# A seven-product MLP step on one Trainium2 core: the order of work where the last up task meets the first down pair

## The chip, the cores and the metric

The kernel runs on one core of one Trainium2 chip. The metric is the device time of one execution in microseconds (us), the median of several runs. Matrix products run on TensorE (PE in the profile; PEld is its weight load), elementwise work on VectorE (DVE), ScalarE (ACT) and GpSimd (POOL); SyncE (SP) issues DMAs. Each engine works through its own list of instructions in order.

## The reference, cut to what matters

A two-layer encoder step over 512 prompt frames and 64 sample frames (576 tokens, model width 1024). Layer 0 mixes by causal pooling, layer 1 by sparse attention; each is followed by a squared-ReLU MLP of width 4096. The change lies in the MLP, which runs once in each layer:

```python
def _mlp(h, w_up, w_down):
    u = jax.nn.relu(h @ w_up)
    return (u * u) @ w_down

def _trunk(x, ...):
    for i in range(DEPTH):                      # DEPTH = 2
        h = _rmsnorm(x, norm_mix[i])
        ...                                     # pooling or attention
        x = x + y.astype(x.dtype)
        x = x + _mlp(_rmsnorm(x, norm_mlp[i]), mlp_w_up[i], mlp_w_down[i]).astype(x.dtype)
    return (_rmsnorm(x, norm_final), ...)
```

## The kernel before

**Layout.** Everything is transposed: 128 features lie on the partitions, 576 tokens in the free dimension, cut into two halves of 288. float32 operands are split in a rounded part and a rest (`upper` is ScalarE's cast, `lower` VectorE's subtraction), and a product is three matmuls: both parts of the data with the weights' rounded part, the data's rounded part with the weights' rest.

**Seven products.** A pair of weight blocks times the two token halves is a 2 by 2 block product; `seven` forms it with seven products in place of eight. Seven weight combinations ("weight units") meet seven combinations of the data (the factors b11, t1, t2, b21, t3, b22, t4, in the order in which they are used). A product (`product`) is four K-tiles ("rows" 0 to 3) of three matmuls each, 12 matmuls of 128x288. The results gather in three PSUM banks: b takes b11 and t2, then t3, then t4; c takes t1, then b22; a starts as ScalarE's copy of b11 out of bank b (L530) and takes b21. Between two products of one bank an engine must read the bank: `on.c`, `on.b`, `on.lo0`, `on.hi1`, `on.hi0`, `on.lo1` name these reads.

**Up and down.** The hidden width is done in four chunks. Chunk 0 goes up by plain products. For chunks 1 to 3 there are four up tasks (class `Up`, data from `xs` and `xt`), whose outputs are scaled, rectified, squared (`relu`, L592 on VectorE, then the square on ScalarE, L451) and combined to the seven factors of the next stage in a tile v; their parts go to a tile u. Then come four down pairs (class `Down`), whose rows 0 to 3 are the u tiles of the four up tasks, and which add to the residual x (L559). In the last chunk of the last layer there are three down pairs, and a plain ending (`last`) for the rest.

**The transition.** The last up task of a chunk (`self.final`) makes row 3 of all seven factors. The first down pair after it (`late`) does rows 0 to 2 of t1 and t2 first. There are six such transitions, three in each layer. In the up task, `hi1` adds the saved t1 part of bank c to bank b after t3 (L609) and so frees bank b for t4; `hi0` does the same for bank c (L615); `lo0` reads bank a; `lo1` reads bank b after t4. All four hang on VectorE. v has one buffer, u has four.

**What sets the order.** In this part no order is written out. A scheduler with estimated durations picks, for each engine, the next instruction that it takes to be ready, in the order of the program where several are. Weight units are made by a generator: `ahead()` asks for one more (ScalarE's cast L181, VectorE's subtraction L182, and between them the sums L260 and L264 for the combinations), up to five ahead of use. So the casts and subtractions of weights stand in the same lists as the work on v and u. SyncE and GpSimd issue the weights' DMAs as their buffers come free.

Of the kernel before, what the change touches and what calls it, by code (L numbers as in the profile page):

```python
# [22 lines left out]
HT = T // 2  # L23
# [33 lines left out]
def pool_dsa_kernel(ctx: ExitStack, tc: tile.TileContext, a, o):  # L57
# [339 lines left out]
    def mlp(layer, gi, late=0, end=None):  # L397
# [69 lines left out]
                    phase["u"].tile([P, 7, 2, HT], F32R, tag="u", bufs=4, name=uid("u")))  # L467

        def upper(u, v, f):
            act.copy(u[:, f, 0], v[:, f])  # L470

        def lower(u, v, f):
            dve.tensor_tensor(u[:, f, 1], v[:, f], f32(u[:, f, 0]), ALU.subtract)  # L473

        def parts_of(u, v, f):

            upper(u, v, f)
            lower(u, v, f)

        def first_sum(v):  # L480
            dve.tensor_tensor(v[:, 2], v[:, 4], v[:, 1], ALU.subtract)

        def middle_sums(v):
            dve.scalar_tensor_tensor(v[:, 3], v[:, 5], -1.0, v[:, 2], ALU.mult, ALU.subtract)
            dve.tensor_tensor(v[:, 1], v[:, 5], v[:, 1], ALU.subtract)

        def last_sum(v):
# [8 lines left out]
        def product(bank, w, operand, factor, js, first=False):  # L496
            for j in js:
                wh, wl = (t[:, j * P:(j + 1) * P] for t in w)
                uh, ul = (operand(j, factor, part) for part in range(2))
                for i, (wt, ut) in enumerate(((wh, uh), (wh, ul), (wl, uh))):  # L500
                    pe.matmul(bank[:, :HT], wt, ut, start=first and j == 0 and i == 0, stop=j == 3 and i == 2,  # L501
                              skip_group_check=True)

        tasks = [0]

        def ahead(n=1):

            how["sub"] = dve
            for _ in range(n):
                if len(ready) < LEAD:  # L510
                    u = next(units, None)
                    if u is not None:
                        ready.append(u)

# [5 lines left out]
        def seven(operand, late, on):  # L520


            b, a_, c = (psum1(t) for t in "bac")
            on.banks = [t[:, :HT] for t in (a_, b, c)]
            w = take()
            product(b, w, operand, "b11", rows, True)
            tasks[0] += 1
            if tasks[0] <= SEEDED:
                pe.matmul(a_[:, :HT], w[0][:, :P], operand(0, "b11", 0), start=True, stop=True, skip_group_check=True)
            act.copy(a_[:, :HT], b[:, :HT])  # L530
            ahead()
            w1 = take()
            if late:
                w2 = take()
                product(c, w1, operand, "t1", rows[:3], True)
                product(b, w2, operand, "t2", rows[:3])
                product(c, w1, operand, "t1", rows[3:])
                on.c()
                ahead()
                product(b, w2, operand, "t2", rows[3:])  # L540
            else:
                product(c, w1, operand, "t1", rows, True)
                on.c()
                ahead()
                product(b, take(), operand, "t2", rows)
            on.b()
            ahead()
            for bank, factor, then in ((a_, "b21", on.lo0), (b, "t3", on.hi1), (c, "b22", on.hi0), (b, "t4", on.lo1)):
                product(bank, take(), operand, factor, rows)
                then()  # L550

        class Down:


            def __init__(self, q):
                self.lo, self.hi = ([x[2 * q + i][:, c0:c0 + HT] for i in range(2)] for c0 in (HT, 0))

            def update(self, to, bank, op):
                dve.tensor_tensor(to, to, self.banks[bank], op)  # L559

            def c(self):
                self.update(self.hi[1], 2, ALU.subtract)

            def b(self):
                self.update(self.hi[0], 1, ALU.add)
# [16 lines left out]

        class Up:


            def __init__(self, c, j):
                self.at, self.final = (c, j), j == half - 1
# [18 lines left out]

            def hi1(self):
                v = self.v
                dve.tensor_tensor(v[:, 5], self.banks[1], snap[:, 0], ALU.add)  # L609
                self.relu(5, v[:, 5], ALU.min, 0)  # L610
                ahead()

            def hi0(self):
                v = self.v
                dve.tensor_tensor(v[:, 1], self.banks[2], snap[:, 1], ALU.add)  # L615
                self.relu(1, v[:, 1], ALU.max, 0)
                if end and self.at[0] == 3:
                    left_over(self.at[1], v[:, 1])
                parts_of(self.u, v, slice(5 if self.final else 4, 6))
                first_sum(v)  # L620
                middle_sums(v)

            def lo1(self):
                v = self.v
                self.relu(6, self.banks[1], ALU.min, 1)
                if not self.final:
                    ahead()
                parts_of(self.u, v, slice(1, 4))
                last_sum(v)
                if not self.final:  # L630
                    ahead()
                parts_of(self.u, v, slice(0, 7, 6))
                if self.final:
                    ahead(2)

        def spread():

# [76 lines left out]
        if end:  # L714
            rest = []
            for j in range(half):
                if j % 2 == 0:
                    t = x_sums_tile()
                rest.append(t[:, j % 2])
                split(rest[j], parked[j // 2][:, j % 2, :HT])  # L720
            b11, b22, b21 = ([u[:, FACTORS.index(f)] for u in us] for f in ("b11", "b22", "b21"))
            end([rest + b22, b11 + b21])

# [856 lines left out]
```

## Time and profile before

| what | value |
|---|---|
| median of 3 runs | 1086.31 us (1084.51 to 1087.21) |
| the profiled execution's own time | 1086.18 us |
| its span, first to last instruction | 1084.4 us |
| PE, busy | 1052.2 us, 97% |
| DVE, busy | 905.4 us, 83% |
| ACT, busy | 627.7 us, 58% |
| POOL, busy | 263.9 us, 24% |
| mean granted TensorE clock | 0.994 |

The page of the profile gives busy times by engine, the chain of work that ended last, and the costliest groups of instructions. The views of the trace list waits by engine (who waited for whom, total, times, longest), instructions in order of time with the idle time ahead of them in brackets, and busy times with the granted clock in stretches of the span. A matmul's listed length is about 0.29 us, but matmuls follow each other every 0.13 us; the end of one is modelled.

### The profile page before, as it was taken

The numbers are of one execution on the slowest core, as the hardware profiler recorded it, in microseconds if no ns is written. First come the engines' busy times: TensorE is split into PE (matmuls) and PEld (weight loads), VectorE is DVE, ScalarE is ACT, GpSimd is POOL, SyncE is SP. The second block draws the span as 40 slices with busy tenths as digits, with TensorE's granted clock in tenths as the row PEclk, the third lists the DMA queues.
The fourth block names the chain that finished last, engine by engine and source line by source line (L and its number), as shares of the span: only waits on it lengthen the run. The fifth ranks groups of instructions, "written<-read, shape, count | busy, mean of one in ns | idle before, by whom it ended". The sixth has DMA issues, their size and how long they took to land.

```text
span 1084.4 us, 21653 instructions
## 1 busy us (share of the span) xinstructions
PE 1052.2 (97%) x7942; PEld 1024.4 (94%) x7942; DVE 905.4 (83%) x1837; ACT 627.7 (58%) x1240; POOL 263.9 (24%) x285
## 2 busy tenths in 40 slices
PE   9999999999999999999989999999999999999996
PEld 8999999999999999999979888999999999999895
DVE  7889889879978987869998944689889879979974
ACT  8556457447546654444477776456467447547641
POOL 3200111111111100227687892000111111111001
PEclk9999999999999999999999999999999999999998
DMA  8233776676676654456642454443775776676512
GB/s 252 91 100 89 173 163 160 162 164 165 154 165 166 156 161 165 126 155 186 200 113 66 136 161 127 126 108 89 175 162 150 172 167 164 152 170 157 128 50 88
DMA packets 94460, 157.66 MB, mean 145 GB/s; under 512 B 13730, under 2 KB 25297, under 8 KB 94353
## 3 DMA queue, kind: packets, MB, share of 16 engines
q1 hardware_dynamic: 68720, 109.80, 33.1%
q0 software_dynamic: 15840, 28.84, 17.4%
q10 hardware_dynamic: 9792, 17.63, 5.3%
q8 instruction: 62, 1.02, 0.4%
q14 instruction: 46, 0.37, 0.1%
HBM read 141.15 MB, written 10.89 MB: 140 GB/s over the span
## 4 chain that ended last, share of the span: by engine, by line
PE 78%; DVE 8%; DMA 4%; ACT 3%; issue 3%; POOL 2%; SPq 1%; DVEq 0%; POOLq 0%; ACTq 0%
PE b L501 29%; PE c L501 15%; PE up L305 9%; PE a L501 7%; PE pj L305 5%; PE wo L305 2%; PE wa L305 2%; DVE wl L182 2%; PE pb L1005 1%; PE pt L1304 1%; PE sc L1278 1%; PE o L1336 1%; PE dn L305 1%; DMA raw<-in_w_in 1%; DMA raw<-in_w_down 1%
## 5 line engine op out<-in xcount | busy, mean ns | idle before, releaser
L181 ACT CAST wh<-raw 128x512 fp32r<-128x512 f32 (+1 forms) x316 | 194.8, 620 | 250.8 <-PE b L501 84.4
L182 DVE TENSOR_TENSOR wl<-raw,wh 128x512 fp32r<-128x512 f32 (+1 forms) x294 | 206.1, 703 | 38.6 <-ACT wh L181 29.2
L501 PE MATMUL b<-u,wh 128*128 128x288 f32 x992 | 202.2, 296 | 3.6 <-ACT a L530 3.2
L501 PEld LDWEIGHTS b<-u,wh 128*128 128x128 f32 x992 | 159.0, 188 | 6.0 <-ACT a L530 6.0
L181 ACT CAST wh<-sum 128x512 fp32r<-128x512 f32 x165 | 101.7, 620 | 81.3 <-PE b L501 42.3
L501 PE MATMUL b<-u,wl 128*128 128x288 f32 x496 | 145.3, 295 | 0.0
L182 DVE TENSOR_TENSOR wl<-sum,wh 128x512 fp32r<-128x512 f32 x165 | 111.9, 687 | 26.3 <-ACT wh L181 24.0
L238 POOL DMA_DIRECT2D sum<-in_w_down x31 | 27.1, 891 | 329.0 <-DVE u L473 119.3
L501 PE MATMUL c<-u,wh 128*128 128x288 f32 x496 | 102.8, 296 | 0.1
L501 PEld LDWEIGHTS b<-u,wl 128*128 128x128 f32 x496 | 92.9, 188 | 0.0
L305 PE MATMUL up<-xs,wh 128*128 128x288 f32 x512 | 89.6, 296 | 0.9 <-DVE x L1471 0.8
L501 PE MATMUL b<-xt,wh 128*128 128x288 f32 x384 | 78.2, 297 | 6.7 <-DVE v L609 6.7
L473 DVE TENSOR_TENSOR u<-v,u 128x864 fp32r<-128x864 f32 (+2 forms) x100 | 81.7, 824 | 0.5 <-ACT u L470 0.5
L501 PEld LDWEIGHTS c<-u,wh 128*128 128x128 f32 x496 | 79.9, 188 | 1.3 <-DVE x L559 1.3
L501 PE MATMUL b<-xs,wh 128*128 128x288 f32 x384 | 77.2, 294 | 0.0
L305 PEld LDWEIGHTS up<-xs,wh 128*128 128x128 f32 x512 | 74.6, 188 | 2.0 <-ACT wh L181 1.0
L470 ACT CAST u<-v 128x864 fp32r<-128x864 f32 (+2 forms) x100 | 72.6, 729 | 4.3 <-DVE v L488 3.4
L501 PE MATMUL c<-u,wl 128*128 128x288 f32 x248 | 73.1, 295 | 0.0
L238 POOL DMA_DIRECT2D sum<-in_w_up x24 | 20.7, 863 | 211.5 <-DVE wl L182 120.5
L501 PEld LDWEIGHTS b<-xt,wh 128*128 128x128 f32 x384 | 61.5, 188 | 8.1 <-DVE v L609 8.1
L305 PE MATMUL pj<-xs,wh 128*128 128x288 f32 x352 | 61.3, 295 | 0.0
L501 PEld LDWEIGHTS b<-xs,wh 128*128 128x128 f32 x384 | 61.2, 188 | 0.0
(289 smaller groups left out, 2722.3 us busy)
## 6 DMA issues: line engine op xcount, KB each, us to landing
raw<-in_w_up SPq DMA_DIRECT2D x128, 256.0 KB, 3.0
raw<-in_w_down SPq DMA_DIRECT2D x128, 256.0 KB, 2.9
raw<-in_w_o ACTq DMA_DIRECT2D x32, 256.0 KB, 3.1
sum<-in_w_down SPq DMA_DIRECT2D x31, 256.0 KB, 2.8
sum<-in_w_down POOLq DMA_DIRECT2D x31, 256.0 KB, 4.8
raw<-in_w_down POOLq DMA_DIRECT2D x31, 256.0 KB, 5.1
raw<-in_w_in ACTq DMA_DIRECT2D x30, 256.0 KB, 3.4
sum<-in_w_up SPq DMA_DIRECT2D x24, 256.0 KB, 2.9
```

The source lines that it names most:

```text
L181: act.copy(h, src)
L182: how["sub"].tensor_tensor(l, src, f32(h), ALU.subtract)
L238: pool.dma_start(s1, odd[:, 512:], accum_op=ALU.add)
L305: pe.matmul(pt[h][:, :m] if isinstance(pt, tuple) else pt[:, h, :m], wt, xs[k][:, part, c:c + m], start=(k == 0 and i == 0), stop=(k == n ...
L470: act.copy(u[:, f, 0], v[:, f])
L473: dve.tensor_tensor(u[:, f, 1], v[:, f], f32(u[:, f, 0]), ALU.subtract)
L501: pe.matmul(bank[:, :HT], wt, ut, start=first and j == 0 and i == 0, stop=j == 3 and i == 2, skip_group_check=True)
L1005: pe.matmul(pt[:, c0:c0 + rhs.shape[1]], lhs, rhs, start=n == 0, stop=n == len(steps) - 1)
L1278: pe.matmul(pt[:, hh, :nw], q[:, 2 * s + hh], ks[g][:, part, :nw], start=part == 0, stop=part == 1)
L1304: pe.transpose(pp[:, c:c + P], pr[:, hh, kt * P:(kt + 1) * P], ident)
L1336: pe.matmul(o[64 * hh:64 * hh + 64, s * P:(s + 1) * P], V[:, kt, vs], pT[:, c:c + P], start=kt == 0, stop=kt == i)
```

## The change

Four things change in `seven` and `Up`, all for the last up task of a chunk and the down pair behind it:

1. `hi1` of the last up task: ScalarE copies bank b into v (new, L649), and VectorE adds the saved part to that copy in place of reading the bank.
2. `parted`: the next down pair's first product (b11) is queued behind the last matmul of the last up task's t3; for the second down pair it is queued behind the late pair's b22.
3. `lo1` of the last up task makes the parts of factors t1, t2 (slice 2:4) and b21 (6:7) first. The sums and parts of t4 and t3 (`rest`: `side_sum`, `last_sum`, slice 0:2) wait until the late down pair's `on.c`.
4. `gates`, `kept`: weight units that are asked for meanwhile have their casts and subtractions queued behind those factor parts; so have, in the last chunk, the splits for the ending. `tc.issue_after(ins)` makes each instruction in its block follow `ins` on the engine of `ins`; other engines are left free.

```diff
         def product(bank, w, operand, factor, js, first=False):
...
+            return ins
+        @contextmanager
+        def behind(instructions):
+            with ExitStack() as st:
+                for ins in instructions:
+                    st.enter_context(tc.issue_after(ins))
+                yield
         def ahead(n=1):
...
-                    u = next(units, None)
+                    with behind(gates):
+                        u = next(units, None)
         def seven(operand, late, on):
...
-            product(b, w, operand, "b11", rows, True)
+            with behind([parted.pop()] if parted else []):
+                product(b, w, operand, "b11", rows, True)
...
-                on.c()
+                first = on.c()
                 ahead()
                 product(b, w2, operand, "t2", rows[3:])
+                on.b()
+                if left:
+                    with tc.issue_after(first.ins):
+                        left.pop().rest()
+                    gates.append(first.ins)
+                    kept[:] = gates
+                ahead()
...
-                product(bank, take(), operand, factor, rows)
+                ins = product(bank, take(), operand, factor, rows)
+                if factor == "t3" and on.final or factor == "b22" and late and gates:
+                    parted.append(ins.ins)
                 then()
+            if late:
+                gates.clear()
         class Up:
+            def rest(self):
+                side_sum(self.v)
+                last_sum(self.v)
+                parts_of(self.u, self.v, slice(0, 2))
             def hi1(self):
                 v = self.v
-                dve.tensor_tensor(v[:, 5], self.banks[1], snap[:, 0], ALU.add)
+                if self.final:
+                    act.copy(v[:, 5], self.banks[1])
+                dve.tensor_tensor(v[:, 5], v[:, 5] if self.final else self.banks[1], snap[:, 0], ALU.add)
             def hi0(self):
...
-                middle_sums(v)
+                middle_sum(v)
+                if not self.final:
+                    side_sum(v)
             def lo1(self):
                 v = self.v
                 self.relu(6, self.banks[1], ALU.min, 1)
-                if not self.final:
-                    ahead()
+                if self.final:
+                    casts = [upper(self.u, v, f).ins for f in (slice(2, 4), slice(6, 7))]
+                    factors = lower(self.u, v, slice(2, 4))
+                    lower(self.u, v, slice(6, 7))
+                    ahead(2)
+                    gates[:] = [factors.ins, *casts]
+                    left.append(self)
+                    return
+                ahead()
                 parts_of(self.u, v, slice(1, 4))
                 last_sum(v)
-                if not self.final:
-                    ahead()
+                ahead()
                 parts_of(self.u, v, slice(0, 7, 6))
-                if self.final:
-                    ahead(2)
...
-                split(rest[j], parked[j // 2][:, j % 2, :HT])
+                with behind(kept):
+                    split(rest[j], parked[j // 2][:, j % 2, :HT])
```

Three places show how the lists change, all at the first transition of layer 0. Names carry buffer numbers; a row is one instruction, or as many equal ones as its x says.

**PE, from t3 to t4 of the last up task.** b_2328 is the up task's bank b, filled from xs in t3 and from xt in t4; b_2483 (in the changed kernel b_2482) is bank b of the next down pair, filled from the u tiles in b11. Before:

```order
L501 MATMUL b_2483<-u_2172,wh_2403 128x288 x2
L501 MATMUL b_2483<-u_2172,wl_2404 128x288
L501 MATMUL b_2328<-xs_642,wh_2344 128x288 x2
L501 MATMUL b_2328<-xs_642,wl_2345 128x288
L501 MATMUL b_2328<-xs_645,wh_2344 128x288 x2
L501 MATMUL b_2328<-xs_645,wl_2345 128x288
L501 MATMUL b_2328<-xs_648,wh_2344 128x288 x2
L501 MATMUL b_2328<-xs_648,wl_2345 128x288
L501 MATMUL b_2328<-xs_651,wh_2344 128x288 x2
L501 MATMUL b_2328<-xs_651,wl_2345 128x288
L501 MATMUL b_2328<-xt_983,wh_2380 128x288 x2
L501 MATMUL b_2328<-xt_983,wl_2381 128x288
```

The same place in the changed kernel:

```order
L507 MATMUL b_2328<-xs_651,wh_2344 128x288 x2
L507 MATMUL b_2328<-xs_651,wl_2345 128x288
L507 MATMUL b_2482<-u_1862,wh_2403 128x288 x2
L507 MATMUL b_2482<-u_1862,wl_2404 128x288
L507 MATMUL b_2482<-u_2017,wh_2403 128x288 x2
L507 MATMUL b_2482<-u_2017,wl_2404 128x288
L507 MATMUL b_2482<-u_2172,wh_2403 128x288 x2
L507 MATMUL b_2482<-u_2172,wl_2404 128x288
L507 MATMUL b_2328<-xt_983,wh_2380 128x288 x2
L507 MATMUL b_2328<-xt_983,wl_2381 128x288
```

The nine matmuls of the down pair's b11 (rows 0 to 2) stood ahead of t3; now they stand between t3 and t4.

**ACT, from the last up task's squares to the first down pair's copy.** v_2326 and u_2327 belong to the last up task; wh_ are weight units; a_2484 <- b_2483 is the copy of the down pair's b11. Before:

```order
L181 CAST wh_2499<-raw_2229 128x512
L451 ACTIVATE v_2326<-v_2326 128x288
L470 CAST u_2327<-v_2326 128x288
L451 ACTIVATE v_2326<-v_2326 128x288 x2
L181 CAST wh_2527<-sum_2401 128x512
L470 CAST u_2327<-v_2326 128x288
L181 CAST wh_2535<-raw_2252 128x512
L530 COPY a_2484<-b_2483 128x288
L451 ACTIVATE v_2326<-v_2326 128x288
L470 CAST u_2327<-v_2326 128x3x288
L470 CAST u_2327<-v_2326 128x2x288
```

In the changed kernel:

```order
L649 COPY v_2326<-b_2328 128x288
L451 ACTIVATE v_2326<-v_2326 128x288
L470 CAST u_2327<-v_2326 128x288
L451 ACTIVATE v_2326<-v_2326 128x288 x2
L470 CAST u_2327<-v_2326 128x288
L451 ACTIVATE v_2326<-v_2326 128x288
L551 COPY a_2483<-b_2482 128x288
L470 CAST u_2327<-v_2326 128x288
L470 CAST u_2327<-v_2326 128x2x288
L181 CAST wh_2498<-raw_2229 128x512
L181 CAST wh_2526<-sum_2401 128x512
L181 CAST wh_2538<-raw_2252 128x512
```

The copy of bank b into v is new at the head; the three casts of weight units have moved behind the factor parts, and the copy for bank a stands behind the last square instead of behind a cast.

**PE, row 3 of the first down pair.** a, b and c are the down pair's banks, u_2327 is row 3. Before:

```order
L501 MATMUL c_2485<-u_2327,wh_2426 128x288
L501 MATMUL b_2483<-u_2327,wh_2469 128x288
L501 MATMUL a_2484<-u_2327,wh_2473 128x288
L501 MATMUL c_2485<-u_2327,wh_2426 128x288
L501 MATMUL c_2485<-u_2327,wl_2427 128x288
L501 MATMUL b_2483<-u_2327,wh_2469 128x288
L501 MATMUL b_2483<-u_2327,wl_2470 128x288
L501 MATMUL a_2484<-u_2327,wh_2473 128x288
L501 MATMUL a_2484<-u_2327,wl_2474 128x288
L501 MATMUL c_2485<-u_1862,wh_2527 128x288 x2
```

In the changed kernel:

```order
L507 MATMUL a_2483<-u_2327,wh_2472 128x288 x2
L507 MATMUL a_2483<-u_2327,wl_2473 128x288
L507 MATMUL c_2484<-u_2327,wh_2427 128x288
L507 MATMUL b_2482<-u_2327,wh_2468 128x288
L507 MATMUL c_2484<-u_2327,wh_2427 128x288
L507 MATMUL c_2484<-u_2327,wl_2428 128x288
L507 MATMUL b_2482<-u_2327,wh_2468 128x288
L507 MATMUL b_2482<-u_2327,wl_2469 128x288
L507 MATMUL c_2484<-u_1862,wh_2526 128x288 x2
```

Bank a's three matmuls have moved from the end to the head, so that two matmuls, not four, lie between the last one of t1 in bank c and the first one of b22 in the same bank.

More of the change, by code (lines that the diff above doesn't have):

```diff
@@ L469, in upper @@
         def upper(u, v, f):
-            act.copy(u[:, f, 0], v[:, f])
+            return act.copy(u[:, f, 0], v[:, f])
         def lower(u, v, f):
-            dve.tensor_tensor(u[:, f, 1], v[:, f], f32(u[:, f, 0]), ALU.subtract)
+            return dve.tensor_tensor(u[:, f, 1], v[:, f], f32(u[:, f, 0]), ALU.subtract)
         def parts_of(u, v, f):
             upper(u, v, f)
-            lower(u, v, f)
+            return lower(u, v, f)
         def first_sum(v):
@@ L483, in middle_sums, with middle_sum, side_sum @@
         def middle_sums(v):
+            middle_sum(v)
+            side_sum(v)
+        def middle_sum(v):
             dve.scalar_tensor_tensor(v[:, 3], v[:, 5], -1.0, v[:, 2], ALU.mult, ALU.subtract)
+        def side_sum(v):
             dve.tensor_tensor(v[:, 1], v[:, 5], v[:, 1], ALU.subtract)
@@ L500, in product @@
                 for i, (wt, ut) in enumerate(((wh, uh), (wh, ul), (wl, uh))):
-                    pe.matmul(bank[:, :HT], wt, ut, start=first and j == 0 and i == 0, stop=j == 3 and i == 2,
-                              skip_group_check=True)
+                    ins = pe.matmul(bank[:, :HT], wt, ut, start=first and j == 0 and i == 0, stop=j == 3 and i == 2,
+                                    skip_group_check=True)
+            return ins
         tasks = [0]
+        parted = []
+        gates = []
+        left = []
+        kept = []
+        @contextmanager
[4 more added lines that the diff above has]
+                yield
         def ahead(n=1):
@@ L545, in seven @@
                 product(b, take(), operand, "t2", rows)
-            on.b()
-            ahead()
+                on.b()
+                ahead()
             for bank, factor, then in ((a_, "b21", on.lo0), (b, "t3", on.hi1), (c, "b22", on.hi0), (b, "t4", on.lo1)):
-                product(bank, take(), operand, factor, rows)
+                ins = product(bank, take(), operand, factor, rows)
+                if factor == "t3" and on.final or factor == "b22" and late and gates:
+                    parted.append(ins.ins)
                 then()
+            if late:
+                gates.clear()
         class Down:
+            final = False
             def __init__(self, q):
@@ L558, in update @@
             def update(self, to, bank, op):
-                dve.tensor_tensor(to, to, self.banks[bank], op)
+                return dve.tensor_tensor(to, to, self.banks[bank], op)
             def c(self):
-                self.update(self.hi[1], 2, ALU.subtract)
+                return self.update(self.hi[1], 2, ALU.subtract)
             def b(self):
@@ L620, in hi0 @@
                 first_sum(v)
-                middle_sums(v)
+                middle_sum(v)
+                if not self.final:
+                    side_sum(v)
             def lo1(self):
@@ L625, in lo1 @@
                 self.relu(6, self.banks[1], ALU.min, 1)
-                if not self.final:
-                    ahead()
+                if self.final:
[7 more added lines that the diff above has]
+                ahead()
                 parts_of(self.u, v, slice(1, 4))
                 last_sum(v)
-                if not self.final:
-                    ahead()
+                ahead()
                 parts_of(self.u, v, slice(0, 7, 6))
-                if self.final:
-                    ahead(2)
         def spread():
```

## The prediction

> **What bounds the kernel now.** The page first: PE is busy 97% of the span and carries 78% of the chain that ended last, so the time can only fall where PE waits.
>
> ```profile
> PE 1052.2 (97%) x7942; PEld 1024.4 (94%) x7942; DVE 905.4 (83%) x1837; ACT 627.7 (58%) x1240; POOL 263.9 (24%) x285
> PE 78%; DVE 8%; DMA 4%; ACT 3%; issue 3%; POOL 2%; SPq 1%; DVEq 0%; POOLq 0%; ACTq 0%
> ```
>
> Then the waits of PE by releaser. The two longest are the places that the change touches: the matmul behind `hi1`'s read of bank b (L609), six times, once in each transition, and the one behind ScalarE's copy (L530).
>
> ```profile
> PE b L501 <- DVE v L609: 6.7, 6, 1.2
> PE b L501 <- ACT a L530: 3.2, 7, 1.0
> ```
>
> The first transition in order of time, PE's rows: the down pair's b11 begins at 183.08, t3 ends with the row at 185.73, t4 begins at 187.14 (start, length, in brackets idle time and releaser).
>
> ```profile
> 183.08 0.42 PE L501 MATMUL b<-u,wh 128*128 128x288 f32 x2
> ...
> 185.46 0.43 PE L501 MATMUL b<-xs,wh 128*128 128x288 f32 x2
> 185.73 0.29 PE L501 MATMUL b<-xs,wl 128*128 128x288 f32 x1
> 187.14 0.53 PE L501 MATMUL b<-xt,wh 128*128 128x288 f32 x2 [1.12 <-DVE v L609]
> 187.51 0.30 PE L501 MATMUL b<-xt,wl 128*128 128x288 f32 x1
> ```
>
> Two matmuls take 0.27 us (185.46 to 185.73), so one takes 0.133. From the last of t3 to the first of t4 it is 1.41, that is 1.28 lost, not only the 1.12 of the bracket, which counts from a modelled end. And the two behind the wait take 0.37 (187.14 to 187.51) in place of 0.27: a restart costs 0.10. A wait with an idle of g thus costs about g + 0.26.
>
> VectorE at the same time:
>
> ```profile
> 185.30 0.69 DVE L264 TENSOR_TENSOR sum<-sum,raw 128x512 f32<-128x512 f32 x1
> 185.91 0.45 DVE L592 SCALAR_TENSOR_TENSOR v<-a,rbm 128x288 f32<-128x288 f32 x1
> 186.27 0.45 DVE L615 TENSOR_TENSOR v<-c,snap 128x288 f32<-128x288 f32 x1
> 186.64 0.45 DVE L609 TENSOR_TENSOR v<-b,snap 128x288 f32<-128x288 f32 x1
> 187.00 0.68 DVE L182 TENSOR_TENSOR wl<-raw,wh 128x512 fp32r<-128x512 f32 x1
> ```
>
> No gap stands between them: L609 is late because VectorE has a queue. (Instructions overlap by about 0.09: 185.91 to 186.27 is 0.36 for one of 0.45.)
>
> **Part 1: t3, b11, t4, and the copy of bank b (gain).** From 183.08 both orders do the same 21 matmuls before t4, 21 x 0.133 = 2.80: PE comes to t4 at 185.88. Now t3 is first and its last matmul begins at 183.08 + 11 x 0.133 = 184.55 and ends 0.29 later, at 184.84. ScalarE's copy takes what L530's take, 0.39, and is done near 185.3, 0.6 ahead of need; VectorE's queue no longer matters. So the wait goes wholly: (1.28 + 0.10) x 6 = **8.3 us**.
>
> **Part 2: the copy for bank a (gain).** PE's rows, then ScalarE's:
>
> ```profile
> 190.29 0.29 PE L501 MATMUL c<-u,wl 128*128 128x288 f32 x1
> 190.74 0.54 PE L501 MATMUL b<-u,wh 128*128 128x288 f32 x2 [0.15 <-ACT a L530]
> ```
>
> ```profile
> 189.77 0.62 ACT L181 CAST wh<-raw 128x512 fp32r<-128x512 f32 x1
> 190.29 0.40 ACT L530 COPY a<-b 128x288 f32<-128x288 f32 x1
> ```
>
> A weight cast stood ahead of the copy and now stands behind it. Lost: 0.45 - 0.13 + 0.10 = 0.42, in five transitions 2.1; the sixth is below. Is the copy in time? The groups that I need (by engine, line and shape: count, busy us, mean ns):
>
> ```profile
> L451 ACT ACTIVATE v<-v 128x288 f32<-128x288 f32 x96 | 41.2, 441 | 5.4 <-DVE v L592 5.4
> L470 ACT CAST u<-v 128x576 fp32r<-128x576 f32 x46 | 30.9, 673 | 2.9 <-DVE v L488 2.5
> ...
> L530 ACT COPY a<-b 128x288 f32<-128x288 f32 x55 | 21.5, 392 | 6.2 <-PE b L501 3.7 <-PE a L529 1.5 <-DVE x L559 1.0
> ...
> L470 ACT CAST u<-v 128x288 fp32r<-128x288 f32 x18 | 7.7, 430 | 0.3
> ...
> L473 DVE TENSOR_TENSOR u<-v,u 128x576 fp32r<-128x576 f32 x46 | 34.6, 752 | 0.0
> ```
>
> t4 runs from 185.88 and its last matmul ends near 187.64; VectorE's scaling (0.45) is done at 188.13, the square (0.44) at 188.60, the copy (0.39) at 188.9. PE, behind b11's row 3 (to 187.87) and nine matmuls of t1, needs it at 189.07. The margin is only 0.15, so up to 2.1 us may stay; I take the gain in full, since each length in the chain is a row's.
>
> Row 3 then: casts and subtractions of b21 and t1/t2 (0.43 + 0.67 on ScalarE, then 0.75 on VectorE) put the last of them near 190.8; PE, with 18 more matmuls to do, asks at 191.5 for b21 and 191.9 for the others. Hidden. The postponed t4 and t3 parts are asked for only after t3's first nine matmuls, near 196. The three units that now stand behind the casts follow from 189.9 at 0.53 each on ScalarE and 0.6 on VectorE: t3's is whole at about 191.4, b22's at 192.0, t4's, behind the reads and sums, at 194.4. The first that PE takes up is b22's, near 192.7. Hidden, with 0.7 to spare.
>
> **Part 3: bank c (loss).** b22 may not write bank c until VectorE has read t1 out of it:
>
> ```profile
> 193.79 0.30 PE L501 MATMUL c<-u,wl 128*128 128x288 f32 x1
> ...
> 194.32 0.29 PE L501 MATMUL a<-u,wl 128*128 128x288 f32 x1
> 194.64 0.54 PE L501 MATMUL c<-u,wh 128*128 128x288 f32 x2
> ```
>
> ```profile
> 194.13 0.46 DVE L559 TENSOR_TENSOR x<-x,c 128x288 f32<-128x288 f32 x1 [0.28 <-PE c L501]
> ```
>
> Last matmul in c to first of b22: 0.85. Four matmuls lie between now; with bank a's moved ahead, two. Lost anew: 2 x 0.133 = 0.27, in five transitions **1.35 us**.
>
> **Part 4: the last transition.** There ScalarE and VectorE also split the ending's operands, and PE waits four times:
>
> ```profile
> 1021.39 0.29 PE L501 MATMUL c<-u,wl 128*128 128x288 f32 x1
> 1022.67 0.53 PE L501 MATMUL b<-u,wh 128*128 128x288 f32 x2 [0.99 <-ACT a L530]
> ...
> 1025.30 0.29 PE L501 MATMUL b<-u,wh 128*128 128x288 f32 x1
> 1025.76 0.40 PE L501 MATMUL a<-u,wh 128*128 128x288 f32 x1 [0.17 <-ACT u L470]
> 1026.02 0.40 PE L501 MATMUL c<-u,wh 128*128 128x288 f32 x1
> ...
> 1026.53 0.30 PE L501 MATMUL b<-u,wl 128*128 128x288 f32 x1
> 1027.06 0.41 PE L501 MATMUL a<-u,wh 128*128 128x288 f32 x1 [0.23 <-DVE u L473]
> ```
>
> The copy: 1.28 - 0.13 + 0.10 = 1.25. The others: 0.33 + 0.13 + 0.40 + 0.10 for the last restart = 0.96. Both go, as the splits move behind the factor parts. Two losses come: bank c's, which had six matmuls between and no wait, 0.85 - 3 x 0.133 + 0.10 = 0.55; and in the second down pair, whose t2 now follows its b11 in PE's list with nothing between, while a weight cast (0.62) stands ahead of its copy. End of a matmul 0.29, cast 0.53 net of overlap, copy 0.39, some 0.1 for handing over: 1.3 between starts, 1.2 lost. Between 0.7 (cast done early) and 1.3; I take 1.2, since cast and copy are released by the same matmul. Net 1.25 + 0.96 - 0.55 - 1.2 = **0.5 us**.
>
> **The sum.** 8.3 + 2.1 - 1.35 + 0.5 = 9.5 us. The additional instructions (a copy and one cast more on ScalarE, one subtraction more on VectorE in each transition, about 0.6 and 0.15 us) lie beside PE's matmuls. The profiled execution took 1086.18, 0.13 under the median; its span is 1084.4. 1086.18 - 9.5 = **1076.7 us**.
>
> On the restart, PE's weight loads have this row:
>
> ```profile
> 187.14 0.30 PEld L501 LDWEIGHTS b<-xt,wh 128*128 128x128 f32 x2 [1.35 <-DVE v L609]
> ```
>
> The load waits along with the matmul. [...]
>
> **The rivals.**
>
> *The clock in attention falls elsewhere.* Neighbouring stretches of the attention layer (columns: length, busy time of PE, PEld, DVE, ACT, POOL with instructions, then the granted clock):
>
> ```profile
> 566.60:573.30 6.70, 6.46 (x30) 6.46 (x31) 4.63 (x18) 3.71 (x13) 5.32 (x4) 0.50 0.15 42
> 573.40:580.00 6.60, 6.60 (x55) 6.57 (x53) 6.46 (x22) 5.37 (x17) 2.46 (x4) 1.00 0.29 79
> ```
>
> For 6.7 us the clock is halved and PE does 30 matmuls where 55 follow in as long: 3.3 us lost at most. The change moves attention some 4 us earlier and turns a few of its instructions round, so the stretch may be missing (1073.4) or come twice (1080.0). [...]
>
> *The copy stays late.* If ScalarE runs 0.15 us or more behind my chain, part 2's 2.1 us stay: 1078.8. For: the margin; against: no wait of ScalarE's is left in it but the ones that I counted.
>
> *The idle moves.* Row 3 of t1 and t2 is the end of a chain through both engines that starts at t3; were it 2.6 us later than reckoned (1.1 of slack and 1.5 gained in each transition), nothing would change: 1086. Against: VectorE loses three subtractions of 0.69 and one sum from this stretch.
>
> *Slower: the weight units come late.* Three units of each transition are cast about 4 us later than before, and their raw buffers come free as much later. Below 0.7 us of delay nothing happens; beyond 0.7 + 1.5 = 2.2 us the gain is used up. At 3 us, PE would lose 0.8 x 6 = 4.8 more than it gains: 1091. Against, the page's row of these casts:
>
> ```profile
> L181 ACT CAST wh<-raw 128x512 fp32r<-128x512 f32 (+1 forms) x316 | 194.8, 620 | 250.8 <-PE b L501 84.4
> ```
>
> ScalarE is idle for 250.8 us ahead of them, 84.4 of it until matmuls of bank b give weight buffers back: units are made ahead of need, and PE is what they wait for.
>
> **How the numbers follow.** Forecast 0.62; clock 0.18, half to each side; late copy 0.12; idle moved 0.04; slower 0.04. The predicted time is the forecast's. The range takes in both ends of the clock, 1073.4 and 1080, the late copy, and 1 us for both lesser losses together: 1073.3 to 1081. About 0.3%, 3.3 us, is what a measurement of this kernel can tell from no change: faster than 1083.0 has 0.92, within 0.04, slower 0.04.
>
> **What would show it.** In the changed kernel PE's waits should have no row for the read of bank b by t4 (L609's successor, L649 or L650) and none for the copy in the first five transitions. A wait of PE's bank c matmuls for VectorE's x (L593), six times about 0.3 us of bracket, should be new, and one of about 1 us for the copy (L551) near the end. If PE waits for wl (L182) or u (L473) at the transitions, parts 1 and 2 have only moved their idle time; if the stretches of attention differ by over 2 us, the difference is not this change's own.

## The result, and the profile after

The changed kernel takes 1077.91 us (median of 6 runs, 1076.55 to 1079.77) against 1086.28 for the kernel before on the same chips: a ratio of 0.9927, 95% interval 0.9911 to 0.9942. Forecast were 1076.7 us and 1073.3 to 1081.0. The profiled execution took 1077.92, its span is 1076.1.

The page of the changed kernel, busy times and shares of the chain that ended last: PE carries 82% of it in place of 78%.

```profile
PE 1049.3 (98%) x7942; PEld 1023.4 (95%) x7942; DVE 905.3 (84%) x1843; ACT 630.8 (59%) x1252; POOL 264.7 (25%) x285
PE 82%; DVE 6%; DMA 4%; POOL 3%; issue 2%; ACT 2%; SPq 0%; DVEq 0%; POOLq 0%; ACTq 0%
```

PE's waits by releaser (us in total, times, longest). Of the two rows at the top of the list of before, the one for t4 is gone. Of the copy's five waits, four of about 0.48 stand at the start of the layers, two in each, and the fifth is the new one of 0.9 near the end. Both kernels have the four: they made 1.9 of the 3.2 us listed for the copy before, so less of that row lay at the transitions than its place in the list suggests. A row for bank c is new.

```profile
PE b L507 <- ACT a L551: 2.8, 5, 0.9
PE c L507 <- ACT wh L181: 2.2, 6, 0.4
```

The first transition in order of time. PE (start, length): t3 ends with the row at 184.38, b11 goes on, t4 follows at 185.69 with no wait.

```profile
184.38 0.29 PE L507 MATMUL b<-xs,wl 128*128 128x288 f32 x1
...
185.69 0.43 PE L507 MATMUL b<-xt,wh 128*128 128x288 f32 x2
...
187.28 0.62 PE L507 MATMUL b<-u,wh 128*128 128x288 f32 x2
187.74 0.29 PE L507 MATMUL b<-u,wl 128*128 128x288 f32 x1
```

ScalarE's two copies there, of bank b and then for bank a, and VectorE at the same time:

```profile
184.71 0.40 ACT L649 COPY v<-b 128x288 f32<-128x288 f32 x1 [1.09 <-PE b L507]
...
188.33 0.40 ACT L551 COPY a<-b 128x288 f32<-128x288 f32 x1
```

```profile
185.89 0.45 DVE L650 TENSOR_TENSOR v<-v,snap 128x288 f32<-128x288 f32 x1
186.26 0.82 DVE L631 SCALAR_TENSOR_TENSOR v<-v,rbm 128x288 f32<-128x288 f32 x2
187.00 0.45 DVE L473 TENSOR_TENSOR u<-v,u 128x288 fp32r<-128x288 f32 x1
```

The copy of bank b ends at 185.11, 0.58 ahead of t4. One loss is new here: b11's last row takes 0.46 from 187.28 to 187.74 where two matmuls take 0.27, because VectorE's subtraction of that row (L473) ends at 187.45, behind two scalings. That is 0.19 here, 0.11 to 0.20 in the six transitions and 1.0 in all, and the list of waits, which leaves out so short a stop, does not show it.

Then bank c: PE, VectorE and ScalarE.

```profile
192.24 0.29 PE L507 MATMUL c<-u,wl 128*128 128x288 f32 x1
...
193.17 0.51 PE L507 MATMUL c<-u,wh 128*128 128x288 f32 x2 [0.37 <-ACT wh L181]
193.52 0.29 PE L507 MATMUL c<-u,wl 128*128 128x288 f32 x1
```

```profile
192.57 0.46 DVE L593 TENSOR_TENSOR x<-x,c 128x288 f32<-128x288 f32 x1
...
195.85 0.68 DVE L182 TENSOR_TENSOR wl<-sum,wh 128x512 fp32r<-128x512 f32 x1
```

```profile
190.18 0.62 ACT L181 CAST wh<-sum 128x512 fp32r<-128x512 f32 x1
...
192.44 0.62 ACT L181 CAST wh<-sum 128x512 fp32r<-128x512 f32 x1
```

From the last matmul in c to b22 it is 0.93. The profile names a weight cast, that of 192.44, which ends at 193.06; VectorE's read of bank c ends at 193.03, 0.03 earlier. That cast can't be b22's own: its lower part (L182) is made at 195.85, while b22 multiplies by its lower part at 193.52; b22's is the one of 190.18, long done. The forecast had named VectorE; e4 below decides.

Where the time went by stage. The marks are PE's rows at the first wait for the copy in each layer, the first product of attention and the first of the ending, here of the changed kernel:

```profile
98.73 0.40 PE L507 MATMUL b<-u,wh 128*128 128x288 f32 x1 [0.48 <-ACT a L551]
...
410.15 0.43 PE L305 MATMUL pj<-xs,wh 128*128 128x288 f32 x2
...
743.18 0.40 PE L507 MATMUL b<-u,wh 128*128 128x288 f32 x1 [0.49 <-ACT a L551]
...
1043.01 0.43 PE L305 MATMUL dn<-xt,wh 128*128 128x288 f32 x2
```

The same marks in all profiles of this study, as differences in us ("layers" is the first plus the second):

| kernel | median | first layer | between | second layer | layers |
|---|---|---|---|---|---|
| before | 1086.3 | 315.22 | 333.35 | 303.83 | 619.05 |
| changed | 1077.9 | 311.43 | 333.03 | 299.83 | 611.26 |
| e1, b11 first again | 1080.7 | 312.63 | 333.10 | 300.69 | 613.32 |
| e2, no copy of bank b | 1078.0 | 312.27 | 331.69 | 301.13 | 613.40 |
| e3, units free | 1088.1 | 316.35 | 333.04 | 302.13 | 618.48 |
| e4, bank c covered | 1076.4 | 310.39 | 332.56 | 299.25 | 609.64 |
| e5, gates and rest only | 1077.8 | 312.35 | 330.06 | 301.24 | 613.59 |
| e6, order and copy only | 1088.6 | 319.62 | 330.63 | 305.49 | 625.11 |
| e7, rest at once | 1089.1 | 318.49 | 331.93 | 304.80 | 623.29 |
| e8, e4 and b11's row first | 1075.6 | 309.86 | 333.38 | 298.64 | 608.50 |
| e9, changed again | 1077.9 | 311.37 | 332.26 | 299.91 | 611.28 |
| e10, e5 again | 1080.8 | 312.37 | 331.11 | 301.33 | 613.70 |

Of the span's 8.3 us the layers hold 7.8. A layer repeats within 0.1 us from one execution to another (e9, e10); the stretch between, with attention in it, moves by about one for the same program (e9, e10) and by up to three over all kernels.

### The profile page after: what moved, and what is told of

Read it like the earlier page. It is cut to its first block, busy times and chain, and to the rows that moved or that the text cites. A ratio compares the mean times of both kernels' runs of the same rounds, so it can differ in the third digit from the quotient of the medians.

```text
span 1076.1 us, 21652 instructions
## 1 busy us (share of the span) xinstructions
PE 1049.3 (98%) x7942; PEld 1023.4 (95%) x7942; DVE 905.3 (84%) x1843; ACT 630.8 (59%) x1252; POOL 264.7 (25%) x285
## 4 chain that ended last, share of the span: by engine, by line
PE 82%; DVE 6%; DMA 4%; POOL 3%; issue 2%; ACT 2%; SPq 0%; DVEq 0%; POOLq 0%; ACTq 0%
PE b L507 33%; PE c L507 16%; PE up L305 9%; PE a L507 8%; PE wo L305 3%; PE pj L305 3%; PE wa L305 2%; PE sc L1326 1%; PE pb L1053 1%; PE pt L1352 1%; PE dn L305 1%; PE o L1384 1%; DVE m L1278 1%; DVE work L1279 1%; DVE wl L182 1%
## 5 line engine op out<-in xcount | busy, mean ns | idle before, releaser
L182 DVE TENSOR_TENSOR wl<-raw,wh 128x512 fp32r<-128x512 f32 (+1 forms) x294 | 204.9, 700 | 36.8 <-ACT wh L181 28.5
L182 DVE TENSOR_TENSOR wl<-sum,wh 128x512 fp32r<-128x512 f32 x165 | 112.3, 687 | 19.9 <-ACT wh L181 18.4
L473 DVE TENSOR_TENSOR u<-v,u 128x576 fp32r<-128x576 f32 (+3 forms) x106 | 83.0, 786 | 2.0 <-ACT u L470 1.6
L470 ACT CAST u<-v 128x576 fp32r<-128x576 f32 (+3 forms) x106 | 73.7, 699 | 6.4 <-DVE v L494 5.4
```

What stands on the lines that cost most here:

```text
L182: how["sub"].tensor_tensor(l, src, f32(h), ALU.subtract)
L470: return act.copy(u[:, f, 0], v[:, f])
L473: return dve.tensor_tensor(u[:, f, 1], v[:, f], f32(u[:, f, 0]), ALU.subtract)
```

## The experiments

Four parts make up the change: the **order** (t3 ahead of the next b11), the **copy** of bank b, the **gates** on the weight units, and the **rest**, postponed behind the read of t1. e1, e2 and e3 undo order, copy and gates one at a time; e7 undoes the rest, and with it the gate that the rest sets for later units. In e1 and e5, b11 of the second down pair stays queued behind b22, and e6 has no such order; what this half of point 2 is worth was not tried by itself.

### e1: the order undone

```diff
-                if factor == "t3" and on.final or factor == "b22" and late and gates:
+                if factor == "b22" and late and gates:
```

> The changed kernel with one part undone: the next down pair's b11 no longer has to follow t3 (ScalarE's copy, the weight units behind the casts and the postponed rest stay). Theory 1, as predicted (order and copy together free t4, the rest is small change): t3 is the last product ahead of t4 again; from the start of its last matmul to t4 stand its 0.29, a hand-over of 0.05, the copy's 0.39 and 0.05 again, 0.78 in place of 0.133, with 0.10 for the restart 0.75 lost in each of six transitions, 4.5 us: 1082.4 us, and PE's waits show a row of bank b for the copy (L649) six times, about 0.6. Rival (the units behind the casts and the postponed rest carry the gain, since they empty both queues): t3 late or early is the same to VectorE, little changes, 1078 to 1079.

Measured: 1080.65 us, ratio to before 0.9950 [0.9936, 0.9965], between the two expectations. PE's waits of e1, and its rows at bank c:

```profile
PE b L507 <- ACT v L649: 2.9, 6, 0.5
```

```profile
193.24 0.29 PE L507 MATMUL a<-u,wl 128*128 128x288 f32 x1
193.64 0.51 PE L507 MATMUL c<-u,wh 128*128 128x288 f32 x2
193.98 0.29 PE L507 MATMUL c<-u,wl 128*128 128x288 f32 x1
```

t4's wait came as theory 1 said (0.5 of bracket, 0.75 with start and restart), but the layers grew by only 2.06, not 4.5: PE is later, so b22, with a matmul before it and two behind (193.24 to 193.98, 0.74 in place of 3 x 0.133), loses 0.34; in the changed kernel it loses 0.93 - 0.40 = 0.53 and 0.08 by the restart (193.17 to 193.52), 0.61. And b11's row no longer stops (0.16 on average). 0.75 - 0.27 - 0.16 = 0.32, times six 1.9. These waits cover one another: what is taken from one comes back in the next.

### e2: the copy of bank b undone

```diff
-                if self.final:
-                    act.copy(v[:, 5], self.banks[1])
-                dve.tensor_tensor(v[:, 5], v[:, 5] if self.final else self.banks[1], snap[:, 0], ALU.add)
+                dve.tensor_tensor(v[:, 5], self.banks[1], snap[:, 0], ALU.add)
```

> The changed kernel without ScalarE's copy of bank b: VectorE adds t3 straight out of the bank, as before the change; order, gates and postponed rest stay. Theory 1 (VectorE's queue is what held t4, the copy gets round it): in the changed kernel VectorE came to its add at 185.89, 0.78 after the copy had ended (185.11). t4 starts where that add ends, 186.39 in place of 185.69, and pays a restart: 0.8 in each of six transitions, 4.8 us, 1082.7 us, with six waits of bank b for VectorE's add of about 0.55. Rival (t3 ahead of b11 is enough by itself, since VectorE's queue has become short): below 1079.

Measured: 1078.04 us, 0.9927 [0.9912, 0.9942]: by the median nothing is lost. But the six waits of theory 1 are there (PE's waits of e2):

```profile
PE b L507 <- DVE v L648: 3.1, 6, 0.5
```

and the layers are 2.14 longer; the stretch between them is 1.34 shorter in this profile, and the rest of the difference lies ahead of the first layer. So neither reading holds whole: the copy is worth 2.1 us in the layers, not 4.8, for the reason of e1.

### e3: the weight units free

```diff
-                    with behind(gates):
+                    with behind([]):
```

> The changed kernel without the gates on the weight units: casts and subtractions of weights may again be issued between the casts of the factors; order, copy and postponed rest stay, and the ending's splits keep their place. Theory 1, as predicted: the gates only bring the copy for bank a forward, 0.42 x 5 and about 0.5 at the last transition, 2.1 to 2.6 us; some of it is offset by a smaller wait at bank c: 1080.0 us (1078.5 to 1080.5), with five waits of 0.15 for that copy. Rival (the parts work only together): with b11 begun later and ended later, three weight casts of 0.53 on ScalarE and three subtractions of 0.6 on VectorE stand ahead of the casts and subtractions of b11's and t1's last row, so PE waits there over 1 us in each of six transitions: 1085 to 1090, the whole gain, and PE's waits name u (L470, L473) at banks b and c.

Measured: 1088.11 us, 1.0030 [1.0013, 1.0047]: slower than before the change. Theory 1's 1080 falls, and the rival's 1085 to 1090 holds; the layers are 7.2 longer than the changed kernel's, some 1.3 of it put down to a stretch at half clock (an estimate, last section); a further 1.6 came in the ending and was not followed up. PE's rows, then ScalarE's, then VectorE's:

```profile
187.37 0.29 PE L507 MATMUL b<-xt,wl 128*128 128x288 f32 x1
188.57 0.40 PE L507 MATMUL b<-u,wh 128*128 128x288 f32 x1 [0.91 <-ACT u L470]
189.90 0.40 PE L507 MATMUL b<-u,wh 128*128 128x288 f32 x1 [0.93 <-DVE u L473]
```

```profile
187.57 0.62 ACT L181 CAST wh<-sum 128x512 fp32r<-128x512 f32 x1 [0.66 <-PE b L507]
188.10 0.43 ACT L470 CAST u<-v 128x288 fp32r<-128x288 f32 x1
```

```profile
188.42 0.68 DVE L182 TENSOR_TENSOR wl<-sum,wh 128x512 fp32r<-128x512 f32 x1
...
189.39 0.45 DVE L473 TENSOR_TENSOR u<-v,u 128x288 fp32r<-128x288 f32 x1
```

t4 waits no longer, yet b11's last row waits twice. The weight cast at the head of ScalarE's queue stood idle for 0.66 until a matmul of bank b gave its buffer back, and the cast that PE needs next (L470) stood behind it. The weight casts ahead of the factors cost more than their 0.53: they tie ScalarE to PE's own progress.

### e4: more matmuls between t1 and b22

```diff
+                w = take()
+                if held and factor == "b21":
+                    product(bank, w, operand, factor, rows[:3])
+                    with behind([last.ins]):
+                        product(bank, w, operand, factor, rows[3:])
...
```

("last" is t2's last matmul, "held" is true in the first down pair of a transition.)

> The changed kernel with one order more: in the first down pair of each transition the last row's three matmuls of bank a come behind the last row of banks b and c, so that five matmuls in place of two lie between the last one of t1 in bank c and b22, which overwrites that bank. Theory 1 (b22 waits for VectorE's read of bank c, which ended 0.146 ahead of b22's start in all six places): from the last matmul in c to b22 0.93 is needed, 6 x 0.133 = 0.80 is covered, so of 0.61 lost some 0.2 stay: 0.4 x 6 = 2.4 us gained, 1075.5 us. Rival (b22 waits for ScalarE's weight cast, which the profile's wait list names, six times, 2.2 us): that cast began only when a matmul of bank a had given its weights back, and bank a now ends 0.40 later, so the wait grows by as much: 1080.3 us.

Measured: 1076.39 us, 0.9909 [0.9895, 0.9924]; the row for bank c is gone from PE's waits. PE, VectorE and ScalarE in e4:

```profile
192.13 0.30 PE L507 MATMUL a<-u,wl 128*128 128x288 f32 x1
192.37 0.51 PE L507 MATMUL c<-u,wh 128*128 128x288 f32 x2
192.72 0.29 PE L507 MATMUL c<-u,wl 128*128 128x288 f32 x1
```

```profile
191.77 0.45 DVE L602 TENSOR_TENSOR x<-x,c 128x288 f32<-128x288 f32 x1 [0.43 <-PE c L507]
```

```profile
192.17 0.61 ACT L181 CAST wh<-sum 128x512 fp32r<-128x512 f32 x1
```

b22 loses 0.24 + 0.35 - 0.40 = 0.19 in place of 0.61, and starts 0.15 behind the end of VectorE's read, as in the changed kernel (0.14). The weight cast that the profile had named is here the one from 192.17 to 192.78: b22 starts at 192.37, while it is still running, so b22 does not wait for it. That b22 waits for VectorE is shown; the rival's 1080.3 and its longer wait did not come, and the releaser in the profile's list was the wrong one of two. The layers gained 1.62 rather than 2.4: in the last transition three new stops (brackets of 0.36 for L182 and 0.40 for L473, and a shorter one) cost 1.5 in place of the 1.19 lost behind the copy; what else is missing was not followed up.

### e5 and e6: gates and rest alone, order and copy alone

e5 is the changed kernel with the diffs of e1 and e2 both applied. e6 is the kernel before with order and copy added:

```diff
+                if parted:
+                    st.enter_context(tc.issue_after(parted.pop()))
...
+                if factor == "t3" and on.final:
+                    parted.append(ins.ins)
...
-                dve.tensor_tensor(v[:, 5], self.banks[1], snap[:, 0], ALU.add)
+                if self.final:
+                    act.copy(v[:, 5], self.banks[1])
+                dve.tensor_tensor(v[:, 5], v[:, 5] if self.final else self.banks[1], snap[:, 0], ALU.add)
```

> The changed kernel with both the order of t3 and b11 and ScalarE's copy of bank b undone: only the gates on the weight units and the postponed rest are left of the change. Theory 1, as predicted (order and copy bring 8.3 us, the gates 2.1): t4's wait of 1.28 + 0.10 stays, 1085 us. Theory 2, from the first four runs (the gates and the postponed rest empty the queues, and most of the gain hangs on that; order and copy are worth little one at a time): VectorE comes to t3 as soon as it is done, 0.29 + 0.05 + 0.45 + 0.05 from its last matmul to t4, 0.81 lost with the restart where the changed kernel loses none, but PE is later by as much at bank c and at b11's last row, so that some 0.5 of it comes back: 2 to 4 us above the changed kernel, 1080 to 1082.

> The kernel before with only the two edits on which the forecast put 8.3 us: t3 ahead of the next down pair's b11, and ScalarE's copy of bank b; weight units are free and no part of the rest is postponed. Theory 1, as predicted: 1086.3 - 8.3 = 1078 us. Theory 2 (t4's wait only moves, to the casts and subtractions of b11's last row, which stand behind weight units on both engines): no gain, 1085 to 1089 us, no wait of t4 and in its place two waits per transition of bank b's matmuls for u (L470 and L473) of about 0.9 each.

Measured: e5 1077.83 us, 0.9931 [0.9913, 0.9950]; e6 1088.55 us, 1.0026 [1.0013, 1.0039]. Theory 1 misses both, by 7 and by 10.5 us, on opposite sides. Theory 2 holds for e6; for e5 its 1080 to 1082 is missed here too, while the repetition (e10) falls into it. The waits of e5 and of e6:

```profile
PE b L507 <- DVE v L648: 3.3, 6, 0.6
```

```profile
PE b L501 <- DVE u L473: 5.7, 6, 1.2
PE b L501 <- ACT u L470: 5.5, 6, 0.9
```

In e5 t4 waits half as long as before (0.55 in place of 1.12) though neither of the edits meant for it is there, and the layers gain 5.5 of the 7.8 us. In e6 t4 does not wait, and the wait stands at b11's last row, longer. Of the 6.1 us by which e6's layers are longer than before, about 3.9 (3 x 1.3) are put down to three stretches at half clock (an estimate, last section), and the other 2.2 are there without them.

### e7: the rest at once

```diff
-                if left:
-                    with tc.issue_after(first.ins):
-                        left.pop().rest()
-                    gates.append(first.ins)
-                    kept[:] = gates
+                kept[:] = gates
...
-                    left.append(self)
+                    side_sum(v)
+                    last_sum(v)
+                    parts_of(self.u, v, slice(0, 2))
```

This also lets later units go ahead of the read of t1.

> The changed kernel with the rest not postponed: side sum, last sum and the parts of t4 and t3 are made straight behind the other parts, ahead of the weight units that are still gated, and not behind VectorE's read of t1. Theory 1, as predicted (the postponed parts cost nothing and bring nothing but room): within 2 us of the changed kernel, 1077 to 1080. Theory 2 (the postponing is needed, since whatever stands between the parts of t1 and t2 and VectorE's read of bank c delays b22, and so does whatever delays the gated units): two sums of 0.37 net and a subtraction of 0.66 net stand ahead of that read, 1.4 us, and as much ahead of the first gated unit; PE waits 1.4 to 2 us more in each of six transitions, 1086 to 1090 us.

Measured: 1089.06 us, 1.0031 [1.0018, 1.0044]. PE's waits of e7, and VectorE:

```profile
PE c L507 <- DVE x L589: 12.1, 6, 2.3
```

```profile
193.25 0.68 DVE L182 TENSOR_TENSOR wl<-raw,wh 128x512 fp32r<-128x512 f32 x1
193.85 0.75 DVE L473 TENSOR_TENSOR u<-v,u 128x576 fp32r<-128x576 f32 x1
...
194.88 0.44 DVE L589 TENSOR_TENSOR x<-x,c 128x288 f32<-128x288 f32 x1
```

The read of bank c comes at 194.88 in place of 192.57 (0.7 of that is this execution's later start of the layer), and b22 waits 2 us, within what theory 2 said. No run tells apart what is the rest's and what the units'. VectorE's list shows the size of both: ahead of that read it holds, beyond what the changed kernel has there, the rest's two sums and its subtraction (0.73 + 0.67) and a sum and a subtraction of weights (0.60 each), 1.4 and 1.2 us.

### e8: e4, and b11's last row first

```diff
-                    parts_of(self.u, self.v, slice(4, 5))
+                    self.b11 = parts_of(self.u, self.v, slice(4, 5))
...
-                self.relu(1, v[:, 1], ALU.max, 0)
+                with behind([self.b11.ins] if self.final else []):
+                    self.relu(1, v[:, 1], ALU.max, 0)
```

> The kernel with bank a's last row behind those of banks b and c, with one order more: VectorE subtracts b11's last row ahead of its scaling of the seventh product's neighbour (L631 for factor 1) in place of behind it. In the changed kernel PE stalls there, two starts 0.218 and 0.239 apart in place of 0.133, 0.19 in each of six transitions. Theory 1 (the stall is the place of that subtraction in VectorE's queue): 0.37 earlier, the stall goes, 0.19 x 6 = 1.1 us, 1075.3 us. Rival (the scaling that now comes 0.37 later leads to the square that stands ahead of the copy for bank a, which had 0.29 to spare; PE also comes 0.19 earlier): the wait turns up at that copy, 0.37 - 0.29 + 0.19 = 0.27 and a restart, and nothing is gained or up to 1 us is lost, 1076.4 to 1077.5, with six short waits of bank b for the copy (L551).

Measured: 1075.59 us, 0.9903 [0.9888, 0.9918], the fastest of the study. VectorE subtracts b11's row at 186.27 now, between the scalings, and PE runs on:

```profile
186.81 0.43 PE L507 MATMUL b<-u,wh 128*128 128x288 f32 x2
187.08 0.30 PE L507 MATMUL b<-u,wl 128*128 128x288 f32 x1
```

186.81 to 187.08 is 0.27, no stop. The layers gain 1.14 on e4, theory 1's 1.1 (the stops at this row had taken 0.98 in e4; the rest came in the last transition); no wait for the copy appears.

### e9 and e10: the changed kernel and e5 once more

> The changed kernel once more, word for word, with a profile of its own. Open is why the kernel with gates and postponed rest alone takes as long (1077.8) as the changed one (1077.9), though its two layers, from the first wait for the copy to the attention layer or to the last product, are 2.3 us longer in its profile (613.6 against 611.3): between the layers it is 3.0 us shorter (330.1 against 333.0). Theory 1 (the stretch between the layers is the execution's, by where its half clock falls): the stretch differs from 333.0 by a us or more in this profile, anywhere from 330 to 333.4, the layers are 611.3 again within 0.3, and the median lies about 2 us under that of the gates alone when both run side by side, 1077.5 against 1079.8. Theory 2 (the stretch is the kernel's, by the order of its instructions): 333.0 again within 0.4, and equal medians, 1077.9 and 1077.9.

> The kernel with gates and postponed rest alone once more, word for word, beside the changed kernel. Theory 1 (the stretch between the layers is the execution's): it differs from 330.1 by a us or more, the layers are 613.6 again within 0.3, and the median is about 1079.8, some 2 us above that of the changed kernel. Theory 2 (it is the kernel's): 330.1 again within 0.4 and 1077.9, equal to the changed kernel; order and copy then gain 2.3 us in the layers and the order that the scheduler gives the attention layer along with them costs it again.

Measured side by side: 1077.88 us (0.9927 [0.9912, 0.9942]) and 1080.83 us (0.9956 [0.9943, 0.9969]). Both layers repeat (611.28 and 613.70). The stretch between came 0.77 and 1.05 away from what it was, near but not all of what theory 1 asked, and stays shorter in e5's program, which suggests that part of it is the kernel's; with two executions of each that is not shown. All runs of both together have medians of 1077.9 (12 runs) and 1079.8 (9 runs): order and copy are worth about 2 us on top of gates and rest, as the layers say (2.3 and 2.4). With so few runs, e5's median in the first comparison could equal the changed kernel's.

## Why the prediction was nearly right in sum, and wrong on what earns it

**Part 1 (t4, 8.3 us).** The wait went wholly in all six transitions (8.2 us by the starts in the kernel before), and t4 came at 185.69 (forecast 185.88). But "VectorE's queue no longer matters" holds for t4 alone, and the gain is not order's and copy's: alone they gain nothing (e6, slower than before by 2.9 us), and without both 5.5 of the layers' 7.8 us remain (e5). Taking t4's wait away gains only once the gates and the postponed rest have cleared the queues for what comes next, and the prediction did not say so: its number held because all four edits were made together, and to that extent it was lucky.

**Part 2 (the gates, 2.1 us).** The copy for bank a was in time, with 0.3 to spare in place of 0.15, and the first five waits for it are gone. The step that failed is what it left out: the gates were valued at that one copy and the last transition's waits, and b11's last row ("behind b11's row 3 (to 187.87)") was taken as free of cost with or without them. Taking the gates away costs 10.2 us by the medians (e3), since that row is then where PE waits. The rival "the idle moves" did name VectorE's three subtractions as work that goes, but for row 3 of t1 and t2 alone, and without a price. The postponed rest was counted at nothing, "hidden"; without it and its gate behind the read of t1 the kernel is 11 us slower (e7), some 1.3 of it a stretch at half clock (last section). Separate prices for edits that clear the same two queues do not add up, though the sum for all four together does.

**Part 3 (bank c, -1.35 us).** Mechanism right (e4), size a little off. Before, b22 lost 0.32 - 0.13 to the wait and 0.10 to the restart, 0.29; now 0.61: 0.32 more, times five 1.6. The mis-sized step is "last matmul in c to first of b22: 0.85", which is 0.93 now (the last section says what differs).

**Part 4 (last transition, +0.5 us).** PE and ScalarE in the changed kernel:

```profile
1022.26 0.29 PE L507 MATMUL b<-u,wl 128*128 128x288 f32 x1
1023.48 0.53 PE L507 MATMUL b<-u,wh 128*128 128x288 f32 x2 [0.92 <-ACT a L551]
1023.85 0.42 PE L507 MATMUL a<-u,wh 128*128 128x288 f32 x2
```

```profile
1022.51 0.62 ACT L181 CAST wh<-raw 128x512 fp32r<-128x512 f32 x1 [0.54 <-PE b L507]
1023.03 0.39 ACT L551 COPY a<-b 128x288 f32<-128x288 f32 x1
```

The cast stands ahead of the copy, and 1.22 - 0.13 + 0.10 = 1.19 is lost: forecast 1.2. Bank c takes 0.61 (forecast 0.55). Net +0.4.

**The term not foreseen** is the stop in b11's last row, 1.0 us over the six transitions, which e8 removes. With it 8.2 + 2.1 - 1.6 + 0.4 - 1.0 = 8.1, where the layers, in which all these places lie, gained 7.8; the 0.3 between was not placed. The forecast's 9.5 was too high by this stop, above all, and by bank c's size.

**The rivals.** Half clock in attention: the changed kernel has one such stretch, as the kernel before has.

```profile
561.40:568.40 7.00, 6.34 (x29) 6.12 (x30) 5.70 (x25) 4.51 (x16) 4.83 (x5) 0.52 0.13 37
```

So it moved nothing in the first comparison. Over all kernels the part between the layers moves by 3.3 us, as much as the rival allowed, but not with the half clock alone: e2's profile shows none (1.00 in every window from 400 to 700) and has 331.69, e5's shows some 3.4 us of it (0.91 over the 20 us from 560) and has 330.06. What else moves it stays open. The weight units did not come late, and the copy for bank a did not either: at the transitions PE's waits have no row for L182, and for the copy only the last one's. Nor did the idle move to row 3 of t1 and t2: there is no row for L470 or L473; 1.0 us of it came back at b11's row.

## What to carry to other kernels

When PE waits on an engine with a full queue, find which work in that queue PE does not need soon and move that; freeing the one instruction that PE waits for passes the wait on to the next in line. Undo each part of a change alone before believing which one earned its gain, and compare stretches that repeat (here two layers, within 0.1 us) where medians of a few runs move by 2 to 3. Where the wait list names one of two releasers that end 0.03 us apart, move one of them.

## What the runs showed of the hardware

**The clock halves after short waits, in some places.** Windows of e6, then of e7 (length, busy time of PE, PEld, DVE, ACT, POOL, then the granted clock):

```profile
187.00:190.50 3.50, 1.67 (x11) 1.29 (x10) 3.40 (x9) 3.09 (x8) 0.00 (x0) 0.99 0.59 201
190.50:194.00 3.50, 3.50 (x17) 3.50 (x16) 3.12 (x6) 1.67 (x3) 0.86 (x1) 0.52 0.24 56
```

```profile
193.00:195.50 2.50, 0.55 (x5) 0.34 (x4) 2.50 (x6) 1.55 (x3) 0.00 (x0) 1.00 0.62 188
195.50:199.00 3.50, 3.50 (x27) 3.50 (x28) 3.50 (x8) 0.62 (x1) 1.75 (x2) 1.00 0.61 178
...
285.00:287.40 2.40, 0.42 (x4) 0.29 (x3) 2.40 (x6) 1.20 (x3) 0.00 (x0) 1.00 0.74 237
287.40:291.00 3.60, 3.60 (x18) 3.60 (x18) 3.31 (x6) 0.62 (x1) 1.75 (x2) 0.53 0.63 163
```

In e6 two waits of 0.9 leave PE busy for 1.67 of 3.5 us, and over the next 3.5 us the granted clock is 0.52: PE does 17 matmuls where e7, at 1.00, does 27 in as long (195.50 to 199.00), so about 10 x 0.133 = 1.3 us are lost on top of the waits. In e7 the clock falls to 0.53 behind a window in which PE is idle for 1.98 us (2.40 - 0.42), and stays at 1.00 behind one with 1.95 (2.50 - 0.55). So the length of the wait alone does not tell where the clock halves; what else does was not shown.

How many such stretches there are is an estimate from the mean clock of the profiled executions: 0.996 in e5 and e10, 0.994 in e3, 0.991 in e6, while all four lose the same 1.7 us to the clock in their windows from 400 to 700, with attention. 0.002 and 0.005 of the span are 2.2 and 5.4 us; one stretch as in e6 loses 0.48 x 3.5 = 1.7 us of full clock. That is about one stretch more in e3 and three more in e6. In the kernel before and in the changed one the clock is 1.00 throughout the layers, with waits there of 1.2 and of 0.9 at most.

**Two waits on one matmul.** Before the change b22 started 0.05 behind the end of VectorE's read (194.13 + 0.46 to 194.64); now it is 0.14 to 0.15 in the changed kernel and in e4. In the trace its first matmul waited for VectorE's semaphore alone before; now it waits for ScalarE's as well, for its weights' cast, which ended 2.2 us before the read (190.18 + 0.62). The two figures repeat wherever b22 stops in these two profiles: 0.055 to 0.056 in the five places of the kernel before, with one wait, and 0.146 to 0.147 in the six of the changed kernel, with two. So a second wait seems to cost 0.09 here even when it is long fulfilled, an estimate from these places; it was not tried by itself.
